# Spacing the steps of scale maxima, moving score maxima of two attention jobs, and giving two elementwise steps to GpSimd in a two-layer hybrid backbone

## The chip, the cores and the metric

The kernel runs on one core of one Trainium2 chip, in one launch. The metric is the device time in microseconds. Before the change the median of three runs is 2726.7 us (2722.78 to 2733.41).

The engines are named as in the profile: PE (TensorE, with its weight loads PEld), DVE (VectorE), ACT (ScalarE), POOL (GpSimd) and SP, whose queue issues nearly all DMAs.

## The reference

Two layers over 2048 latent and 256 context tokens of width 1024. Cut to what is computed:

```python
def hybrid_layer(h, hc, ...):
    lat = split_cols((rms_norm(h, norm_g) * (1.0 + scale) + shift) @ w_in)     # 1024 -> 3584 columns, 15 parts
    cx  = split_cols((rms_norm(hc, norm_g) * (1.0 + scale_c) + shift_c) @ w_in)
    att_l, att_c = gqa_branch(...)      # 4 heads, 2 KV heads, axial rotary, softmax over 2304 keys
    hg_l, hg_c = hgrn_branch(...)       # recurrence, both directions, chunks of 64
    y_conv, y_four, g_att, g_hg = mix_stream(lat, conv_w)   # width-3 convolution; 2-D Fourier; SiLU gates
    y = jnp.concatenate([y_conv, att_l * g_att, hg_l * g_hg, y_four], axis=-1) @ w_out
    h_new = h + gate * y
    # the same for the context stream in layer 0
def attend(qb, k, v):
    s = einsum(q, k) * HEAD_DIM ** -0.5
    p = softmax(s); return einsum(p, v)
# after both layers: rms_norm(h, final_g)
```

## The kernel before

Products that need more than one float16 are made of three float16 products: every operand is split into a high and a low half after it was multiplied by a power of two. That power comes from the largest absolute value of the whole tensor, over all partitions. Its steps are: a maximum along each partition on DVE, a transpose of that column by PE (`rowmax`, L140), a maximum of the row on DVE (L142), a product with ones that spreads the number over all partitions (`spread`, L148), a copy and five small DVE instructions (`pow2`), and then the two split halves (L406 on ACT, L407 on DVE). For the weights `wsplit` does this for each block of 256 columns of `w_in`, 14 blocks a layer.

A layer runs in stages, one after another: the projections and the recurrence (HGRN), its reverse with the Fourier inputs, the Fourier mix, the attention projections, and then four attention jobs. A job is 512 queries. `att_max` forms all scores once with high halves alone and takes their maxima on DVE (L941 on PE into PSUM, L942 on DVE; per job 64 tiles 512 wide and 16 tiles 256 wide). `att_core` forms the scores again transposed, 72 steps per job: two score products (L1016, L1017), the exponential on ACT (L1019), its high half (L1025 on ACT, or L1023 on DVE in the steps that `dve` and `first` name), its low half on DVE (L1026), and four pairs of products with V (L983, L984), which follow four steps later.

Beside the jobs run other streams. Before, in terms of stages: "core 0" is job 0 with the maxima of job 1 and six convolution blocks; "core 1" is job 1 with the maxima of job 2 and the first output tiles; "core 2" is job 2 with the maxima of job 3 and three output tiles; "core 3" is job 3 with four output tiles, and the "tail" is six output tiles (in layer 0 beside the first weights of layer 1). An output tile is 128 tokens: gating (L1266) and splitting of its input (`out_prep`), 48 products 512 wide (L1306), scaling by the gate from PSUM (L1310), the residual add (L1311), and in layer 1 a sum of squares on ACT (L1317). Core 1 begins with `out_open`, which makes the scale of the output's input from six maxima at once (L1599 to L1618).

What sets the order is `weave`: each stream is a generator with a number of units and a share of the stage, and the stream that is furthest behind goes next. A `yield` is a unit's end, so a bare `yield` lets the other streams put their work in between. Instructions then stand in each engine's queue in about that order, and each queue is worked off in order. `paced` makes an instruction wait for the last DVE and ACT instruction recorded before it.

Of the kernel before, what the change touches and what calls it, by code (L numbers as in the profile page):

```python
# [22 lines left out]
D = 1024  # L23
# [49 lines left out]
class Net:  # L73
# [63 lines left out]
    def rowmax(self, a):  # L137
        nc = self.nc
        pt = self.bank("tr")
        nc.tensor.transpose(pt[:1, :128], a, self.id32)  # L140
        m = self.t(self.small, [1, 1], F32, "rowmax")
        nc.vector.tensor_reduce(out=m, in_=pt[:1, :128], axis=AX.X, op=ALU.max)  # L142
        return m

    def spread(self, m):
        nc = self.nc
        pt = self.bank("tr")
        nc.tensor.matmul(pt[:, 0:1], lhsT=self.ones[:1], rhs=m, start=True, stop=True)  # L148
        r = self.t(self.small, [128, 1], F32, "allmax")
        nc.vector.tensor_copy(out=r, in_=pt[:, 0:1])  # L150
        return r
# [23 lines left out]
    def setup(self):  # L175
# [16 lines left out]
        rows = cst.tile([R_N, 128], F32, name="rows")  # L192
# [192 lines left out]
    def wsplit(self, l, b, half, pool=None, pace=False):  # L385
# [532 lines left out]
    def att_fetch(self, job, pool):  # L918
# [4 lines left out]
        Q1 = self.t(pool, [128, 4, 512], F16, "Q1", 2)  # L923
        Q2 = self.t(pool, [66, 4, 512], F16, "Q2", 2)
# [112 lines left out]
    def conv_block(self, l, sb, W, pool):  # L1037
# [33 lines left out]
        th = self.t(pool, [128, 512], F32, "cth", 1)  # L1071
# [187 lines left out]
    def out_prep(self, tt, pool):  # L1259
# [6 lines left out]
        nc.vector.tensor_mul(out=o, in0=o, in1=g)  # L1266
# [10 lines left out]
    def out_tile(self, l, tt, pool):  # L1277
# [23 lines left out]
        for half in range(2):  # L1301
# [9 lines left out]
            nc.vector.tensor_add(out=h[:, c], in0=h[:, c], in1=t)  # L1311
# [38 lines left out]
    def begin(self, pool, nm):  # L1350
# [4 lines left out]
        self.setup()  # L1355
# [20 lines left out]
    def layer(self, l, L, R, tail):  # L1376
# [17 lines left out]
        else:  # L1394
# [11 lines left out]
            weave(tail, (22, start(), 0.2, 0.9))  # L1406
# [5 lines left out]
        with ExitStack() as st:  # L1412
# [3 lines left out]
            if l == 0:  # L1416
                w = [self.wprep(l, b) for b in (8, 9, 10)]
# [29 lines left out]
            for sb in range(1, NS):  # L1447
                weave((33, self.hg_proj(l, sb, hp)), (22, self.hg_levels(l, sb - 1, hp)), (8, norms(sb), 0.3, 1.0), *([(5, self.wprep(l, 13), 0.4, 0.8)] if sb == NS - 1 else []))
# [14 lines left out]
        preps = lambda bs, pool=None: chain(*[(5, self.wprep(l, b, pool, b < 4)) for b in bs])  # L1463
# [6 lines left out]
        with ExitStack() as st:  # L1470
# [33 lines left out]
        jobs[-1]["dve"] = 3  # L1504
# [6 lines left out]
        with ExitStack() as st:  # L1511
# [18 lines left out]
            weave((7, self.att_values(keep, at), 0.02, 0.2), (*chain(*pre, mx(jobs[0])), 0.25, 1.0), part(some[:n]), (*fetch(jobs[1]), 0.6, 0.7))  # L1530
            weave(core(jobs[0]), mx(jobs[1]), part(some[n:]))
# [25 lines left out]
    def out_wmax(self, l):  # L1557
# [14 lines left out]
        self.ows, self.owi = self.pow2(self.allmax(am), self.cst, tag=f"ows{l}")  # L1572
# [14 lines left out]
    def out_open(self, l, pool):  # L1587

        nc = self.nc
        self.gbc = []  # L1590
        for s in range(2 if l < DEPTH - 1 else 1):
            g = self.t(pool, [128, D], F32, f"gbc{s}", 1)
# [8 lines left out]
        pt = self.bank("tr")  # L1601
        nc.tensor.transpose(pt[:6, :128], mx, self.id32)
        m = self.t(self.small, [6, 1], F32, "om6", 1)
        nc.vector.tensor_reduce(out=m, in_=pt[:6, :128], axis=AX.X, op=ALU.max)
        dg = self.t(self.small, [6, 6], F32, "odg", 1)
        nc.vector.tensor_scalar_mul(dg, self.id32[:6, :6], m)
        yield
        pt = self.bank("tr")
        nc.tensor.matmul(pt[:, 0:6], lhsT=self.ones, rhs=dg, start=True, stop=True)
        a = self.t(self.small, [128, 6], F32, "oam", 1)  # L1610
        nc.vector.tensor_copy(out=a, in_=pt[:, 0:6])
# [75 lines left out]
```

## Time and profile before

| | before |
|---|---|
| median of the runs | 2726.7 us |
| the profiled execution, its own time | 2724.91 us |
| its span, first to last instruction | 2721.5 us |
| mean granted TensorE clock | 0.982 |
| busy share of the span: PE, DVE, ACT, POOL | 95%, 79%, 55%, 4% |

The profiled execution is 1.8 us under the median, so differences are taken against 2724.91. A busy share is an average over all stages. A matmul counts as busy from its start to its modelled end, and neighbours overlap, so PE's busy time is read together with the spacing of the starts.

### The profile page before, as it was taken

What the parts mean: (1) busy time and instruction counts of PE and PEld (TensorE: products, weight loads), DVE (VectorE), ACT (ScalarE), POOL (GpSimd) and SP (SyncE); (2) the same over time, 40 slices, a digit from 0 to 9 for tenths busy, and PEclk for the clock granted to TensorE, in tenths of its full rate; (3) what the DMA queues carried; (4) which work ended last, traced back from release to release, by engine and by line L of the source; (5) the groups of instructions that cost most, each with busy time, mean ns of one, the idle gap of its engine ahead of it and who ended that gap; (6) DMA issues with size and microseconds to landing.
All of it is one profiled execution on the core that took longest, in us unless ns stands there. A gap on an engine that the chain in (4) does not pass through costs nothing. (4 is left out here: it accounts for less than half of the span.)

```text
span 2721.5 us, 67137 instructions
## 1 busy us (share of the span) xinstructions
PE 2576.0 (95%) x28046; PEld 1915.2 (70%) x28046; DVE 2147.0 (79%) x4707; ACT 1495.4 (55%) x2789; POOL 105.0 (4%) x108
## 2 busy tenths in 40 slices
PE   6999999999999999999999999999988999999998
PEld 3788877888777875555547888878877787455553
DVE  5888765777698669899877888768678876999885
ACT  2877532322226647798837666423221565879782
POOL 0000001011000000000000000010110000000000
PEclk8999999999999999999999999999999999999999
DMA  6111158353411015224281111344333100423425
GB/s 218 56 49 49 37 187 266 116 152 103 113 38 56 16 45 170 77 72 130 55 247 56 48 49 33 101 131 148 110 92 95 40 25 22 145 79 77 115 52 156
DMA packets 268680, 260.32 MB, mean 96 GB/s; under 512 B 95316, under 2 KB 237656, under 8 KB 268376
## 3 DMA queue, kind: packets, MB, share of 16 engines
q1 hardware_dynamic: 268376, 256.04, 31.5%
q8 instruction: 219, 3.59, 0.5%
q14 instruction: 85, 0.70, 0.1%
HBM read 168.59 MB, written 67.13 MB: 87 GB/s over the span
## 5 line engine op out<-in xcount | busy, mean ns | idle before, releaser
L431 PE MATMUL psmm<-xh,wh 128*128 128x256 f16 x2208 | 608.1, 275 | 7.8 <-DVE xh L357 6.1
L432 PE MATMUL psmm<-xl,wh 128*128 128x256 f16 x2208 | 606.7, 275 | 1.5 <-DVE xl L358 1.5
L433 PE MATMUL psmm<-xh,wl 128*128 128x256 f16 x2208 | 606.5, 275 | 0.7 <-DVE wl L407 0.7
L1019 ACT ACTIVATE aP<-pssc,pshift,ascale 128x512 f32<-128x512 f32 (+1 forms) x584 | 444.6, 778 | 221.6 <-PE pssc L1017 193.2
L445 PE MATMUL psmm<-wh,xh 128*128 128x256 f16 x1664 | 459.1, 276 | 5.6 <-ACT av L818 4.2
L1026 DVE TENSOR_TENSOR apl<-aP,aph 128x512 f16<-128x512 f32 (+1 forms) x584 | 390.2, 681 | 86.8 <-ACT aph L1025 82.6
L446 PE MATMUL psmm<-wl,xh 128*128 128x256 f16 x1664 | 458.4, 275 | 0.0
L447 PE MATMUL psmm<-wh,xl 128*128 128x256 f16 x1664 | 458.2, 275 | 0.0
L942 DVE TENSOR_REDUCE amx<-pstr 128x1 f32<-128x512 f32 (+1 forms) x648 | 391.5, 627 | 46.5 <-PE pstr L941 45.1
L1025 ACT CAST aph<-aP 128x512 f16<-128x512 f32 (+1 forms) x508 | 305.5, 619 | 9.6
L983 PE MATMUL pspv<-V,aph 128*128 128x129 f16 x2320 | 298.7, 221 | 1.4 <-DVE aph L1023 1.2
L984 PE MATMUL pspv<-V,apl 128*128 128x65 f16 x2320 | 269.6, 193 | 4.9 <-DVE apl L1026 3.6
L984 PEld LDWEIGHTS <-apl 128*128 128x128 f16 x2320 | 206.6, 98 | 84.4 <-DVE apl L1026 39.7
L983 PEld LDWEIGHTS <-aph 128*128 128x128 f16 x2320 | 214.6, 97 | 68.5 <-ACT aph L1025 9.4
L431 PEld LDWEIGHTS <-wh 128*128 128x128 f16 x2208 | 217.9, 99 | 59.4 <-issue 7.0
L432 PEld LDWEIGHTS <-wh 128*128 128x128 f16 x2208 | 217.8, 99 | 57.0 <-issue 5.8
L941 PE MATMUL pstr<-K,Q 128*128 128x512 f16 (+1 forms) x648 | 230.0, 362 | 13.3 <-DVE amx L942 8.8
L433 PEld LDWEIGHTS <-wl 128*128 128x128 f16 x2208 | 217.5, 99 | 34.2 <-issue 2.1
L1016 PE MATMUL pssc<-Q,K 128*128 128x512 f16 (+1 forms) x584 | 221.4, 379 | 4.2 <-ACT aP L1019 2.9
L1017 PE MATMUL pssc<-Q,K 66*128 66x512 f16 (+1 forms) x584 | 221.7, 382 | 0.0
L1306 PE MATMUL psmm<-xh,oyh 128*128 128x512 f16 x544 | 206.8, 380 | 1.9 <-DMA oyh<-oa 1.8
L1306 PE MATMUL psmm<-xl,oyh 128*128 128x512 f16 x544 | 206.7, 380 | 0.0
(310 smaller groups left out, 4228.5 us busy)
## 6 DMA issues: line engine op xcount, KB each, us to landing
wst<-w_in SPq DMA_DIRECT2D x56, 512.0 KB
wmod<-w_mod SPq DMA_DIRECT2D x18, 1024.0 KB
d_G<-nh SPq DMA_DIRECT2D x51, 256.0 KB
oo<-d_O SPq DMA_DIRECT2D x34, 384.0 KB
og<-d_G SPq DMA_DIRECT2D x34, 384.0 KB
d_h<-oh SPq DMA_DIRECT2D x18, 512.0 KB
nh<-d_h SPq DMA_DIRECT2D x18, 512.0 KB
nh<-x SPq DMA_DIRECT2D x16, 512.0 KB
```

Of the source, the lines that this page charges most:

```text
L431: nc.tensor.matmul(out, lhsT=wh[:, k, cs], rhs=a, start=(k == 0), stop=False)
L432: nc.tensor.matmul(out, lhsT=wh[:, k, cs], rhs=b, start=False, stop=False)
L433: nc.tensor.matmul(out, lhsT=wl[:, k, cs], rhs=a, start=False, stop=(k == KC - 1))
L445: nc.tensor.matmul(out, lhsT=a, rhs=wh[:, k, :], start=(k == 0), stop=False)
L446: nc.tensor.matmul(out, lhsT=a, rhs=wl[:, k, :], start=False, stop=False)
L447: nc.tensor.matmul(out, lhsT=b, rhs=wh[:, k, :], start=False, stop=(k == KC - 1))
L942: nc.vector.tensor_reduce(out=mx[:, h, j, i : i + 1], in_=ps[:, :w], axis=AX.X, op=ALU.max)
L983: nc.tensor.matmul(pv(j), lhsT=ph[:, t], rhs=self.V[:, s, kv, :], start=st, stop=False, skip_group_check=True)
L984: nc.tensor.matmul(pv(j)[:, 0:65], lhsT=pl[:, t], rhs=self.V[:, s, kv, 0:65], start=False, stop=sp and j % 2 == 1, skip_group_check=True)
L1019: nc.scalar.activation(out=P[:, :n], in_=ps[:, :n], func=AF.Exp, scale=self.ascale, bias=self.pshift)
L1026: nc.vector.tensor_sub(out=pl[:, :n], in0=P[:, :n], in1=ph[:, :n])
L1306: nc.tensor.matmul(ps, lhsT=y, rhs=w, start=(i == 0), stop=(i == len(mms) - 1))
```

## The change

Five things change.

1. `wsplit` has two more bare yields between its steps (not where `quick` is set, that is at the start of layer 0), and `rowmax` is no longer paced; the stream's unit counts grow from 5 to 7. `out_wmax` and `out_open` get such units too. The maximum of the values (`att_vmax`) is taken among the last gate blocks of the attention projections, before it was taken at the start of the stage after.
2. The score maxima of job 2 stand in core 0, behind those of job 1, and those of job 3 in core 1. Q's tiles have three buffers. Job 2, as job 3, now makes 27 of its 72 high halves on DVE (`dve` = 3).
3. The gating product of `out_prep` and the residual add of `out_tile` are GpSimd's.
4. The output tiles are split at 5, 9, 13 (before 5, 8, 12): core 2 gets four, the tail five.
5. Several small tiles lie in other buffers (`rows`, the gate rows, `cth`).

```diff
     def rowmax(self, a):
+        n = a.shape[1]
         pt = self.bank("tr")
-        nc.tensor.transpose(pt[:1, :128], a, self.id32)
+        nc.tensor.transpose(pt[:n, :128], a, self.id32)
...
-    def wsplit(self, l, b, half, pool=None, pace=False):
+    def wsplit(self, l, b, half, pool=None, pace=False, quick=False):
...
         yield
-        with slow():
-            m = self.rowmax(am)
-        yield
+        if not quick:
+            yield
+        m = self.rowmax(am)
+        yield
+        if not quick:
+            yield
...
+    def att_vmax(self):
+        am = self.t(self.small, [128, 1], F32, "vam", 1)
+        self.nc.vector.tensor_reduce(out=am, in_=self.vmax, axis=AX.X, op=ALU.max)
+        yield
+        m = self.rowmax(am)
+        yield
+        self.vscale, self.visc = self.pow2(self.spread(m), self.cst, tag="avs")
+        yield
...
-        Q1 = self.t(pool, [128, 4, 512], F16, "Q1", 2)
-        Q2 = self.t(pool, [66, 4, 512], F16, "Q2", 2)
+        Q1 = self.t(pool, [128, 4, 512], F16, "Q1", 3)
+        Q2 = self.t(pool, [66, 4, 512], F16, "Q2", 3)
...
-        th = self.t(pool, [128, 512], F32, "cth", 1)
+        th = self.t(pool, [128, 512], F32, "cc", 3)
...
-        nc.vector.tensor_mul(out=o, in0=o, in1=g)
+        nc.gpsimd.tensor_tensor(out=o, in0=o, in1=g, op=ALU.mult)
...
-            nc.vector.tensor_add(out=h[:, c], in0=h[:, c], in1=t)
+            nc.gpsimd.tensor_tensor(out=h[:, c], in0=h[:, c], in1=t, op=ALU.add)
...
-            weave(tail, (22, start(), 0.2, 0.9))
+            weave(tail, (30, start(), 0.2, 0.9))
...
-        jobs[-1]["dve"] = 3
+        jobs[-1]["dve"] = jobs[-2]["dve"] = 3
...
-            weave(core(jobs[0]), mx(jobs[1]), part(some[n:]))
+            run(fetch(jobs[2])[1])
+            weave(core(jobs[0]), chain(mx(jobs[1]), mx(jobs[2])), part(some[n:]))
...
-        T = (5, 8, 12)
-        run(fetch(jobs[2])[1])
+        T = (5, 9, 13)
+        run(fetch(jobs[3])[1])
         weave(
             core(jobs[1]),
-            (*mx(jobs[2]), 0.05, 1.0),
-            (*chain((1, self.out_load(l, t0, ou)), *[(1, self.out_weights(k)) for k in (6, 7)], (3, self.out_open(l, ou))), *((0.0, 0.04) if need else (0.055, 0.08))),
-            (*out(range(t0, T[0])), 0.07 if need else 0.09, 1.0),
+            (*mx(jobs[3]), 0.05, 1.0),
+            (*chain(*[(1, self.out_weights(k)) for k in (6, 7)], (4, self.out_open(l, ou)), (1, self.out_load(l, t0, ou))), *((0.0, 0.08) if need else (0.02, 0.11))),
+            (*out(range(t0, T[0])), 0.12 if need else 0.14, 1.0),
         )
-        run(fetch(jobs[3])[1])
-        weave(core(jobs[2]), (*mx(jobs[3]), 0.05, 1.0), out(range(T[0], T[1])))
+        weave(core(jobs[2]), out(range(T[0], T[1])))
```

On PE at the border of core 0 and core 1 of layer 0, before: L1602 is the transpose of the six maxima and L1609 the product that spreads them, L983 and L984 are products with V, L941 score maxima.

```order
L984 MATMUL pspv_14068<-V_10661,apl_14585 128x65
L1602 MATMUL pstr_14684<-id_90,omx_2055_14681 6x128
L1609 MATMUL pstr_14690<-odg_14688,ones 128x6
L941 LDWEIGHTS Q_2040_14628
L941 MATMUL pstr_14756<-K_1393_10659,Q_2040_14628 128x512
```

The two stood next to each other, and ten score-maxima products followed before the next step of the core. After the change the same product (now L155; its transpose, L142, stands 71 rows ahead of it) has core steps (L998 and L999 with V, L1031 and L1032 scores) around it, and the score maxima (L956) alternate with them:

```order
L998 MATMUL pspv_15008<-V_10679,aph_14948 128x129
L999 LDWEIGHTS apl_14949
L999 MATMUL pspv_15008<-V_10679,apl_14949 128x65
L1031 LDWEIGHTS K_1402_10677
L1031 MATMUL pssc_15065<-Q_1519_11403,K_1402_10677 128x512
L155 MATMUL pstr_14983<-odg_14956,ones 128x6
L956 LDWEIGHTS Q_2128_14886
L956 MATMUL pstr_15005<-K_1402_10677,Q_2128_14886 128x512
L1032 LDWEIGHTS K_1403_10678
```

So PE has other work between the transpose and the product that needs DVE's answer. On DVE in the middle of core 2 of layer 0 the maxima (L942) alternated with the low halves (L1026) before:

```order
L1026 TENSOR_TENSOR apl_17253<-aP_17250,aph_17252 128x512
L942 TENSOR_REDUCE amx_16671<-pstr_17256 128x1
L1026 TENSOR_TENSOR apl_17276<-aP_17273,aph_17275 128x512
L942 TENSOR_REDUCE amx_16671<-pstr_17279 128x1
L1026 TENSOR_TENSOR apl_17296<-aP_17293,aph_17295 128x512
```

After it the low halves (L1041) stand there with the high halves that DVE now makes (L1038) and the output tiles' scaling (L1325):

```order
L1041 TENSOR_TENSOR apl_17458<-aP_17455,aph_17457 128x512
L1038 CAST aph_17478<-aP_17476 128x512
L1041 TENSOR_TENSOR apl_17479<-aP_17476,aph_17478 128x512
L1041 TENSOR_TENSOR apl_17499<-aP_17496,aph_17498 128x512
L1041 TENSOR_TENSOR apl_17519<-aP_17516,aph_17518 128x512
```

No maxima are left in core 2. In core 0 of layer 0, DVE had one such reduction for each low half, with a convolution's steps among them; now it has two (L957), as here:

```order
L957 TENSOR_REDUCE amx_13349<-pstr_14036 128x1
L1041 TENSOR_TENSOR apl_14024<-aP_14021,aph_14023 128x512
L957 TENSOR_REDUCE amx_13349<-pstr_14045 128x1
L957 TENSOR_REDUCE amx_13349<-pstr_14071 128x1
L1041 TENSOR_TENSOR apl_14062<-aP_14059,aph_14061 128x512
L957 TENSOR_REDUCE amx_13349<-pstr_14086 128x1
L1082 SCALAR_TENSOR_TENSOR cu_14115<-psmm_13997,ds_9613,cc_13995 128x2x256
```

## Rows read from the trace of the kernel before

**Rows 1.** The page, its first part: busy time, share of the span and number of instructions of each engine.

```profile
PE 2576.0 (95%) x28046; PEld 1915.2 (70%) x28046; DVE 2147.0 (79%) x4707; ACT 1495.4 (55%) x2789; POOL 105.0 (4%) x108
```

**Rows 2.** Busy time in stretches: core 0, 1, 2, 3 and tail of layer 0, then the same of layer 1. Columns: the stretch in us from the span's start, its length, busy us and number of instructions of each engine, the granted clock, DMA's share and GB/s.

```profile
810.00:1008.70 198.70, 198.57 (x1941) 158.44 (x1940) 144.98 (x277) 117.69 (x175) 0.00 (x0) 1.00 0.08 28
1008.70:1147.80 139.10, 131.60 (x1049) 71.58 (x1046) 125.77 (x235) 101.90 (x154) 0.15 (x1) 0.96 0.41 124
1147.80:1259.40 111.60, 109.11 (x949) 61.43 (x946) 103.76 (x188) 96.70 (x154) 0.00 (x0) 1.00 0.29 80
1259.40:1364.00 104.60, 103.43 (x944) 58.44 (x942) 85.02 (x160) 83.12 (x128) 0.00 (x0) 1.00 0.37 102
1364.00:1437.00 73.00, 68.83 (x324) 32.32 (x322) 54.95 (x114) 23.07 (x38) 1.62 (x5) 0.98 0.75 228
2107.50:2310.10 202.60, 202.14 (x1947) 159.59 (x1946) 153.17 (x288) 117.98 (x174) 0.00 (x0) 1.00 0.08 26
2310.10:2427.80 117.70, 111.87 (x951) 61.61 (x948) 114.45 (x222) 98.90 (x159) 1.54 (x2) 0.97 0.36 106
2427.80:2542.60 114.80, 109.31 (x950) 60.86 (x948) 110.77 (x205) 100.06 (x167) 1.96 (x3) 1.00 0.28 78
2542.60:2650.80 108.20, 105.23 (x943) 57.83 (x941) 88.39 (x168) 87.06 (x144) 3.09 (x4) 1.00 0.37 99
2650.80:2721.50 70.70, 62.18 (x289) 27.99 (x286) 38.35 (x64) 15.43 (x35) 3.85 (x7) 0.96 0.53 154
```

**Rows 3.** The waits of PE for the steps of scale maxima: waiting line, what it waited for, us in total, times, the longest. The first two are of the stretch 100 to 760 us (layer 0, past its start), the other two of 1440 to 2107 us (layer 1).

```profile
PE pstr L148 <- DVE rowmax L142: 9.4, 3, 3.8
...
PE pstr L140 <- DVE wam L391: 2.0, 1, 2.0
...
PE pstr L140 <- DVE wam L391: 10.2, 3, 4.5
PE pstr L148 <- DVE rowmax L142: 9.6, 4, 2.7
```

**Rows 4.** The same columns as Rows 2 for eight stretches in which the granted clock fell to its lower level, each right behind a wait of PE: the first of the eight, the two at the start of a core 1, and the sum (length first).

```profile
675.20:678.60 3.40, 3.40 (x19) 2.34 (x17) 2.19 (x6) 0.84 (x2) 0.00 (x0) 0.50 0.41 100
...
1013.10:1023.40 10.30, 8.46 (x21) 2.55 (x20) 9.30 (x26) 2.61 (x4) 0.00 (x0) 0.50 0.77 264
...
2317.00:2323.80 6.80, 5.64 (x14) 1.75 (x13) 5.91 (x18) 1.93 (x3) 0.00 (x0) 0.50 0.90 309
sum 41.00, PE 35.72 PEld 19.79 DVE 33.67 ACT 12.91 POOL 0.00; mean PE 4.47 PEld 2.47 DVE 4.21 ACT 1.61 POOL 0.00
```

**Rows 5.** The timeline of PE in core 0 of layer 0 (start, us, engine, line, operation): a product 512 wide and its successor, one 256 wide and its successor, and the first product with V of three successive pairs (first and last).

```profile
880.01 0.38 PE L1017 MATMUL pssc<-Q,K 66*128 66x512 f16 x1
880.23 0.27 PE L431 MATMUL psmm<-xh,wh 128*128 128x256 f16 x1
...
880.56 0.27 PE L431 MATMUL psmm<-xh,wh 128*128 128x256 f16 x1
880.67 0.27 PE L432 MATMUL psmm<-xl,wh 128*128 128x256 f16 x1
...
882.31 0.22 PE L983 MATMUL pspv<-V,aph 128*128 128x129 f16 x1
...
882.49 0.22 PE L983 MATMUL pspv<-V,aph 128*128 128x129 f16 x1
```

**Rows 6.** Groups by line and shape, over the whole span: line, engine, operation, out<-in, shapes, count, busy us, mean ns of one, idle us before them and what ended it.

```profile
L1026 DVE TENSOR_TENSOR apl<-aP,aph 128x512 f16<-128x512 f32 x576 | 387.2, 685 | 86.8 <-ACT aph L1025 82.6
L942 DVE TENSOR_REDUCE amx<-pstr 128x1 f32<-128x512 f32 x512 | 340.2, 683 | 34.2 <-PE pstr L941 32.9
...
L942 DVE TENSOR_REDUCE amx<-pstr 128x1 f32<-128x256 f32 x136 | 56.2, 416 | 12.3 <-PE pstr L941 12.2
...
L1311 DVE TENSOR_TENSOR oh<-oh,ot 128x512 f32<-128x512 f32 x68 | 46.5, 684 | 0.4
...
L1266 DVE TENSOR_TENSOR oo<-oo,og 128x768 f32<-128x768 f32 x34 | 32.2, 952 | 8.8 <-DMA oo<-d_O 8.7
...
L1023 DVE CAST aph<-aP 128x512 f16<-128x512 f32 x76 | 31.0, 421 | 3.0 <-ACT aP L1019 2.9
```

**Rows 7.** The same columns, the groups of POOL alone. L171 is a power (exponent -0.5).

```profile
L171 POOL TENSOR_TENSOR arr<-arv,mhalf 128x12 f32<-128x12 f32 (+1 forms) x18 | 42.3, 2349 | 369.3 <-DVE arv L169 293.8 <-DVE p2e L123 75.5
L171 POOL TENSOR_TENSOR nrr<-nrv,mhalf 128x1 f32<-128x1 f32 x52 | 31.6, 607 | 1166.9 <-DVE nrv L169 1134.1 <-DVE arc L998 32.8
...
L188 POOL MEMSET cact<- 128x256 f32 x1 | 0.3, 317 | 0.0
...
masks.py:199 POOL TENSOR_SCALAR_AFFINE_SELECT id<-id 128x128 f32<-128x128 f32 x1 | 0.3, 296 | 0.0
```

**Rows 8.** The timeline at the end of the span: the last residual add and the sum of squares behind it.

```profile
2713.74 0.69 DVE L1311 TENSOR_TENSOR oh<-oh,ot 128x512 f32<-128x512 f32 x1
2714.80 0.63 ACT L1317 ACTIVATE ot<-oh 128x512 f32<-128x512 f32 x1 [4.74 <-DVE oh L1311]
```

More of the change, by code (lines that the diff above doesn't have):

```diff
@@ L138, in rowmax @@
         nc = self.nc
+        n = a.shape[1]
         pt = self.bank("tr")
[L140 to L143 removed]
+        nc.tensor.transpose(pt[:n, :128], a, self.id32)
+        m = self.t(self.small, [6, 1], F32, "rowmax")
+        nc.vector.tensor_reduce(out=m[:n], in_=pt[:n, :128], axis=AX.X, op=ALU.max)
+        if n == 1:
+            return m[:1]
+        dg = self.t(self.small, [6, 6], F32, "odg", 1)
+        nc.vector.tensor_scalar_mul(dg[:n, :n], self.id32[:n, :n], m[:n])
+        return dg[:n, :n]
     def spread(self, m):
         nc = self.nc
+        n = m.shape[1]
         pt = self.bank("tr")
[L148 to L150 removed]
+        nc.tensor.matmul(pt[:, 0:n], lhsT=self.ones[:n], rhs=m, start=True, stop=True)
+        r = self.t(self.small, [128, n], F32, f"allmax{n}")
+        nc.vector.tensor_copy(out=r, in_=pt[:, 0:n])
         return r
@@ L191, in setup @@
         self.masks = cst.tile([128, 6, 64], U16, name="masks")
-        rows = cst.tile([R_N, 128], F32, name="rows")
+        rows = self.t(pool, [R_N, 128], F32, "rows", 1)
         def put(r0, src):
@@ L366, in new_x, with wprep @@
         return self.t(pool, [128, KC, n], F16, f"xh{i}", 1), self.t(pool, [128, KC, n], F16, f"xl{i}", 1)
-    def wprep(self, l, b, pool=None, pace=False):
+    def wprep(self, l, b, pool=None, pace=False, quick=False):
         half = self.wload(l, b)
         yield
-        yield from self.wsplit(l, b, half, pool, pace)
+        yield from self.wsplit(l, b, half, pool, pace, quick)
     def wload(self, l, b):
@@ L1362, in begin @@
             if i == 2:
-                run(self.wsplit(0, 7, half))
+                run(self.wsplit(0, 7, half, quick=True))
             run(self.mod_cols(0, x, w[i], mod, pool, "mm"))
@@ L1416, in layer @@
             if l == 0:
-                w = [self.wprep(l, b) for b in (8, 9, 10)]
+                w = [self.wprep(l, b, quick=True) for b in (8, 9, 10)]
                 with self.after(last):
@@ L1490, in layer, with one @@
             self.att_open(l, ab)
+            vm = self.att_vmax()
+            def one(g):
+                next(g)
+                yield
             weave(
@@ L1493, in layer @@
                     merge(gates(6, 0, some[6:]) + gates(11, 256, some[:-3]), [(17, self.att_block(l, sb)) for sb in range(NS)]),
-                    late(), *gates(11, 256, some[-3:]),
+                    late(), *[x for sb in some[-3:] for x in (*gates(11, 256, [sb]), (1, one(vm)))],
                 ),
-                chain((10, self.out_wmax(l)), preps((1, 2, 3, 0), wc)),
+                chain((12, self.out_wmax(l)), preps((1, 2, 3, 0), wc)),
             )
@@ L1529, in layer @@
             part = lambda sbs: chain(*[x for sb in sbs for x in conv[sb]])
-            weave((7, self.att_values(keep, at), 0.02, 0.2), (*chain(*pre, mx(jobs[0])), 0.25, 1.0), part(some[:n]), (*fetch(jobs[1]), 0.6, 0.7))
-            weave(core(jobs[0]), mx(jobs[1]), part(some[n:]))
+            weave((5, self.att_values(keep, at), 0.02, 0.2), (*chain(*pre, mx(jobs[0])), 0.25, 1.0), part(some[:n]), (*fetch(jobs[1]), 0.6, 0.7))
+            run(fetch(jobs[2])[1])
+            weave(core(jobs[0]), chain(mx(jobs[1]), mx(jobs[2])), part(some[n:]))
         wcs.close()
@@ L1571, in out_wmax @@
         nc.vector.tensor_reduce(out=am, in_=mx, axis=AX.X, op=ALU.max)
-        self.ows, self.owi = self.pow2(self.allmax(am), self.cst, tag=f"ows{l}")
+        yield
+        m = self.rowmax(am)
+        yield
+        self.ows, self.owi = self.pow2(self.spread(m), self.cst, tag=f"ows{l}")
         yield
@@ L1600, in out_open @@
         nc.vector.tensor_reduce(out=mx[:, 5:6], in_=self.vmax, axis=AX.X, op=ALU.max)
[L1601 to L1606, printed above, removed]
         yield
[L1608 to L1611, printed above, removed]
+        m = self.rowmax(mx)
+        yield
+        a = self.spread(m)
         b = self.t(self.small, [128, 4], F32, "obd", 1)
```

19 lines of the change are left out of this document (8 added, 11 removed).

## The prediction

> **What bounds the kernel now.** I read the busy shares first. PE is busy 95% of the span, DVE 79%, POOL 4% [rows 1]; so a gain must come from PE's time, and DVE's work is worth something only where it holds PE up. PE's busy time counts overlapping matmuls, so next I took what PE needs at least from the spacing of starts: 0.22 us for a product 512 wide (880.01 to 880.23), 0.11 us for one 256 wide, 0.09 us for a pair of products with V (0.18 us over two pairs) [rows 5]. A step of a core is two 512-wide products and four pairs, 0.80 us, and 72 of them 57.6 us. A job's score maxima are 64 x 0.22 + 16 x 0.11 = 15.8 us. An output tile is 48 x 0.22 = 10.6 us.
>
> Third, the stages [rows 2]. In core 0 PE is busy in 198.6 of 198.7 us and 202.1 of 202.6: PE alone bounds it, and DVE has 28% and 24% to spare. Core 1 needs 57.6 + 15.8 + 5 x 10.6 = 126.4 us of PE in layer 0 and takes 139.1; with three tiles 105.2 and 117.7 in layer 1. Core 2 needs 105.2 and takes 111.6 and 114.8, with DVE busy 93% and 96%. Core 3 needs 57.6 + 4 x 10.6 = 100.0 and takes 104.6 and 108.2. So some 12.6 us are lost in each core 1, 6 to 10 in each core 2, 5 to 8 in each core 3, almost none in core 0.
>
> Last, the waits and the clock. Outside the start of layer 0, PE waits 9.4 + 2.0 + 10.2 + 9.6 = 31.2 us in eleven places for the steps of scale maxima [rows 3]. Behind several of them, and at both starts of core 1, the granted clock is at 0.50 (1.2 GHz) for 41.0 us in all; the two core 1 pieces are 10.3 and 6.8 us of it, so 23.9 us stand elsewhere [rows 4]. At 0.50 PE does half the work, so those 23.9 us cost up to 12.
>
> **The change part by part.** The sum goes against the profiled execution's 2724.9 us, 1.8 under the median.
>
> *Spaced steps.* No instruction is added; between a maximum and the PE instruction that needs it there now stand one or two more units of the other stream. A wait is 0.7 to 4.5 us long, 2.8 on average (31.2 over 11), and a unit of the main stream is at most six products, several of which pass for one of the weights' units; in the order I count 2 to 3 us more PE work between the transpose and the product with ones. I take 28 of the 31.2 us as gone; at worst, if DVE answers later by as much, only a third is gone. What is late next is the split itself, but its weights are used a block later. Of the half-clock 23.9 us I take two thirds of the 12, -8; below that 0, above it -12. The values' maximum lies in the same stretch and is in these numbers.
>
> *Core 0.* It gains 15.8 us of PE in each layer, in full, since PE has no gap there. It also gains 64 x 0.683 + 16 x 0.416 = 50.4 us of reductions [rows 6]: DVE has then 195.4 of 214.5 us (91%) in layer 0 and 203.6 of 218.4 (93%) in layer 1. Core 2 shows what such a share costs: 96% of DVE with 10 us over PE's need, where ACT too was at 87%. ACT is at 59% here, so I take 4 us of collisions: +20 a layer; 16 at least, and 30 where each of six convolution blocks, whose four to six DVE instructions stand in a row, holds PE up for 2.5 us.
>
> *Core 1.* PE's work stays (job 3's maxima for job 2's). Its loss is at the start: in 10.3 us PE ran 21 matmuls at the lower clock while DVE was busy 9.3 us [rows 4], because ten score-maxima products stood ahead of the core's steps and each waited for a reduction of 0.68 us. These now alternate with core steps. DVE also loses 0.952 + 2 x 0.684 = 2.32 us a tile to GpSimd [rows 6], 11.6 us in layer 0 and 7.0 in layer 1. Of the 12.6 us lost I take 9 and 8 back; 3 at least.
>
> *Core 2.* It becomes what core 3 was: 72 steps, 27 high halves on DVE (27 x 0.421 = 11.4 us), four tiles, no maxima. Core 3 takes 104.6 and 108.2 us [rows 2], so core 2 gains 7.0 and 6.6 by that row alone; with 9.3 us less on DVE I take 8 and 10. Core 3 keeps its work and loses the same 9.3 us of DVE, which had 81% there: -1 and -3.
>
> *Tails.* Each loses a tile of 10.6 us. In layer 1 nothing else is there: -10.6, and the last residual add, now GpSimd's, ends later by its extra length (0.69 us on DVE [rows 8], about 1.2 below): -10. In layer 0 the weights of layer 1 run beside it, DVE is at 75% and DMA at 75% [rows 2]; with 2.4 + 5 x 2.3 us less on DVE that goes to PE's length too: -9; if the loads decide, 0.
>
> *GpSimd's length.* No row shows it multiply or add. Its shortest full-width row is a memset, 317 ns for 256 columns, 1.2 ns each; an affine select costs 296 for 128, 2.3 each; the only two-input rows are powers, from 607 ns for one column to 2349 for mostly twelve, 158 ns each [rows 7]. The power's price belongs to the power, since the same engine does 128 columns of the select in half of one column's power; the select is nearest. So 1.8 us for 768 columns and 1.2 for 512, and a tile has P = 4.2 us on POOL, with 2.2 by the memset. A tile comes every 10.6 us at the fastest, so POOL, idle else, keeps up, and the product waits there for its DMA where DVE had waited 8.7 us [rows 6]. Behind the add in layer 1 stands ACT's sum of squares, and behind that the exponentials: 0.5 us more twice a tile, in queues with 13 to 20% idle. I take +2 for all of it. GPSIMD Engine Reference (the Trainium skill), section "Elementwise — side-by-side cycle accounting", gives 4497 ns for an add of 2048 columns, by which P would be an estimated 3.9 us and the sum the same; no run here shows it.
>
> *At nothing:* tiles in other buffers, `rowmax` for six rows (the same instructions as `out_open` had), an earlier fetch of Q (three DMAs on SP, idle at a stage's border).
>
> Sum: layer 0, +20 - 9 - 8 - 1 - 9 = -7; layer 1, +20 - 8 - 10 - 3 - 10 = -11; waits -28, clock -8, GpSimd +2: -52. 2724.9 - 52 = 2673.
>
> **The rivals.** (A) *GpSimd holds DVE up, and the kernel is slower.* If a DVE instruction that reads two SBUF operands can't run beside a GpSimd one that does, each tile gives DVE P instead of taking 2.32 off it. Core 1 then has 114.2 + 5P and 107.5 + 3P of DVE, cores 2 and 3 about 76 + 4P and 79 + 4P. With P = 4.2 core 1 becomes 135 and 120, +5 and +10 on my 130 and 110: 2688. It decides from about P = 8 us (4.5 ns a column): core 1 154 and 132, cores 2 and 3 108 and 111, +65 in all: 2738, slower. For it: L1026, 0.685 us in each of the 72 steps [rows 6], is such an instruction. Against: that P is twice the select's. SBUF — State Buffer (the Trainium skill), "Who interferes with whom", states just this lock: the second of the two blocks until the first ends. Its price by rows is this rival's; the trace of before has only powers of a few columns on POOL there and can't show it.
>
> (B) *DVE becomes core 0's bound.* If it costs there what core 1 of layer 0 shows at the worst, 139.1 us for 125.8 us of DVE [rows 2], a factor 1.106, core 0 is 216 and 225, little over mine; with the 2.5 us at every block as well it is +15 a layer: 2703. For it, the order (two reductions a step, convolution steps between); against, that PE's work in between grows too.
>
> (C) *The waits only move.* If DVE answers later by as much as the added units are long, two thirds of the 28 + 8 stay: 2673 + 24 = 2697. For it: the spaced reductions stand behind the same DVE queue. Against: the waits are short, 4.5 us at most [rows 3].
>
> **How the numbers follow.** The sum has 0.62, A 0.12, B 0.12, C 0.14. A change under 0.5% (13.6 us, 2713 to 2740) is about what a measurement of this kernel can't tell from none. My own case is faster in nearly all its spread (2650 to 2700), B and C at 2697 to 2703 with spreads over 2713 in a third of them, A half within and half slower, and some of A beyond: faster 0.79, same 0.10, slower 0.11. The likeliest case's own range is 2650 to 2697. For 8 in 10 I go down to 2645 (all waits and clock, core 1 at PE's need) and up to 2718, which holds B, C and the mild end of A.
>
> **What would show it.** In the new profile: the waits of PE for `rowmax` and `wam` under 8 us in sum, and few stretches at 0.50; core 0 at 216 to 224 us; core 1 at 130 and 110; core 2 within 2 us of core 3; the last tail at 60. DVE's low halves still 685 ns each beside GpSimd's products of about 1.8 us; if they are longer, or idle DVE stands before them with POOL as the releaser, A is at work. The forecast is wrong if core 0 grows by over 30 us, or if the eleven waits come back under other names.

## The result, and the profile after

The changed kernel takes 2755.2 us (median of 4 runs, 2753.4 to 2762.4), the kernel before on the same chip 2730.1. The ratio is 1.010, with a 95% interval of 1.0068 to 1.0131: slower by one per cent, where 2673 was forecast. The profiled execution took 2757.0 us, its span 2755.2.

The page's first line, which answers to [rows 1]:

```profile
PE 2574.2 (93%) x28046; PEld 1919.1 (70%) x28046; DVE 2175.6 (79%) x4669; ACT 1478.6 (54%) x2725; POOL 269.8 (10%) x210
```

PE has the same matmuls and the same busy time, in a longer span. DVE was to lose work to POOL: it has 38 instructions fewer (the 102 that went to POOL, less 64 high halves of job 2 that came from ACT) and is busy 28.6 us longer. The stages, as in [rows 2] (core 0, 1, 2, 3 and tail of layer 0, then of layer 1; stretch, length, busy us of PE, weight loads, DVE, ACT and POOL, the clock, DMA's share and GB/s):

```profile
813.70:1031.80 218.10, 216.53 (x2024) 166.58 (x2023) 189.37 (x363) 119.27 (x175) 0.00 (x0) 1.00 0.09 30
1031.80:1172.00 140.20, 130.21 (x1049) 71.45 (x1047) 125.52 (x220) 102.25 (x154) 24.94 (x17) 0.99 0.40 115
1172.00:1280.60 108.60, 101.51 (x916) 58.16 (x913) 83.65 (x136) 85.53 (x126) 19.12 (x13) 0.98 0.34 93
1280.60:1392.20 111.60, 101.52 (x942) 59.13 (x940) 83.39 (x140) 85.00 (x125) 19.21 (x12) 1.00 0.31 91
1392.20:1455.00 62.80, 56.93 (x259) 25.99 (x257) 49.30 (x94) 22.16 (x36) 23.40 (x19) 0.95 0.79 243
2114.90:2335.60 220.70, 218.81 (x2028) 167.73 (x2027) 196.70 (x372) 118.68 (x174) 0.00 (x0) 1.00 0.08 26
2335.60:2458.40 122.80, 111.41 (x954) 62.13 (x951) 116.00 (x218) 101.60 (x160) 18.20 (x12) 0.99 0.33 97
2458.40:2573.50 115.10, 103.89 (x917) 59.01 (x915) 88.65 (x148) 88.99 (x142) 22.15 (x17) 0.97 0.31 88
2573.50:2688.90 115.40, 103.81 (x941) 59.30 (x938) 90.40 (x152) 87.71 (x141) 22.23 (x16) 0.99 0.30 88
2688.90:2755.20 66.30, 53.47 (x240) 23.62 (x238) 24.59 (x41) 13.47 (x30) 25.70 (x21) 0.95 0.47 143
```

Core 0 grew by 19.4 and 18.1 us, as forecast. Core 2 has now only 84 to 89 us of DVE, and PE still idles 7 and 11 us in it. Against the forecast, the loss is in the stages in which POOL works and DVE makes low halves, cores 1 to 3, and to a lesser part in the tails. DVE's groups, as in [rows 6] (L1041 is the low half, L957 the score maxima, L1038 DVE's high half, L1285 the low part of a gated tile, L1325 the scaling of an output tile):

```profile
L1041 DVE TENSOR_TENSOR apl<-aP,aph 128x512 f16<-128x512 f32 x576 | 423.3, 741 | 97.1 <-ACT aph L1040 88.4 <-PE pssc L1032 1.3
L957 DVE TENSOR_REDUCE amx<-pstr 128x1 f32<-128x512 f32 x512 | 338.8, 683 | 35.0 <-PE pstr L956 33.7
...
L1038 DVE CAST aph<-aP 128x512 f16<-128x512 f32 x140 | 67.3, 489 | 2.5 <-ACT aP L1034 2.1
...
L1325 DVE TENSOR_TENSOR ot<-psmm,xh 128x512 f32<-128x512 f32 x68 | 46.7, 686 | 25.0 <-PE psmm L1321 24.7
...
L1285 DVE SCALAR_TENSOR_TENSOR ob<-oo,osc,oa 128x768 f16<-128x768 f32 x34 | 41.5, 1224 | 32.5 <-ACT oa L1284 32.5
```

The low half went from 685 to 741 ns and DVE's high half from 421 to 489. The reduction and the scaling, whose large input lies in PSUM, stayed at 683 and 686. POOL's two new groups (compare [rows 7]):

```profile
L1326 POOL TENSOR_TENSOR oh<-oh,ot 128x512 f32<-128x512 f32 x68 | 98.9, 1454 | 524.6 <-DVE ot L1325 485.4 <-DVE ams L964 12.2 <-ACT aph L1040 10.8
L1281 POOL TENSOR_TENSOR oo<-oo,og 128x768 f32<-128x768 f32 x34 | 65.8, 1946 | 405.1 <-DVE apl L1041 321.9 <-DMA oo<-d_O 28.5 <-DMA og<-d_G 20.7
```

So P is 1.95 + 2 x 1.45 = 4.85 us a tile, 0.65 over the 4.2 used. What one tile does in core 3 of layer 0, in the timeline (start, us, engine, line, out<-in; in brackets the idle time ahead and its releaser):

```profile
1296.85 1.58 DVE L1285 SCALAR_TENSOR_TENSOR ob<-oo,osc,oa 128x768 f16<-128x768 f32 x1 [2.67 <-ACT oa L1284]
1297.53 0.38 PE L1031 MATMUL pssc<-Q,K 128*128 128x512 f16 x1 [1.28 <-ACT aP L1034]
...
1297.57 1.98 POOL L1326 TENSOR_TENSOR oh<-oh,ot 128x512 f32<-128x512 f32 x1
...
1298.35 1.75 DVE L1041 TENSOR_TENSOR apl<-aP,aph 128x512 f16<-128x512 f32 x1
...
1300.02 0.41 DVE L1038 CAST aph<-aP 128x512 f16<-128x512 f32 x1
...
1300.15 0.20 PE L999 MATMUL pspv<-V,apl 128*128 128x65 f16 x1 [1.32 <-DVE apl L1041]
...
1300.21 0.78 ACT L1034 ACTIVATE aP<-pssc,pshift,ascale 128x512 f32<-128x512 f32 x1 [0.97 <-DVE apl L1041]
...
1301.28 0.68 DVE L1041 TENSOR_TENSOR apl<-aP,aph 128x512 f16<-128x512 f32 x1
```

POOL's add runs to 1299.55. The low half that starts in it takes 1.75 us and ends 0.55 after it; the next one, with POOL free, takes 0.68. PE (products with V) and ACT (the next exponential, whose buffer the low half still reads) each wait for it by name. PE's two groups that wait, over the span (scores, and products with the low half):

```profile
L999 PE MATMUL pspv<-V,apl 128*128 128x65 f16 x2320 | 269.7, 194 | 16.1 <-DVE apl L1041 15.2
...
L1031 PE MATMUL pssc<-Q,K 128*128 128x512 f16 x576 | 219.9, 382 | 32.6 <-ACT aP L1034 31.6
```

Before, the same waits were 3.6 and 2.9 us. The waits for the steps of scale maxima, which were 31.2 us in [rows 3], did go (stretches 100 to 760 and 1440 to 2114 us):

```profile
PE pstr L142 <- DVE wam L398: 2.6, 1, 2.6
PE pstr L142 <- DVE wam L398: 5.0, 2, 3.7
```

### The profile page after: what moved, and what is told of

It is laid out like the page before. It is cut to its first block, busy times and chain, and to the rows that moved or that the text cites. A ratio compares the mean times of both kernels' runs of the same rounds, so it can differ in the third digit from the quotient of the medians.

```text
span 2755.2 us, 67284 instructions
## 1 busy us (share of the span) xinstructions
PE 2574.2 (93%) x28046; PEld 1919.1 (70%) x28046; DVE 2175.6 (79%) x4669; ACT 1478.6 (54%) x2725; POOL 269.8 (10%) x210
## 5 line engine op out<-in xcount | busy, mean ns | idle before, releaser
L1041 DVE TENSOR_TENSOR apl<-aP,aph 128x512 f16<-128x512 f32 (+1 forms) x584 | 426.3, 737 | 97.1 <-ACT aph L1040 88.4
L957 DVE TENSOR_REDUCE amx<-pstr 128x1 f32<-128x512 f32 (+1 forms) x648 | 390.5, 627 | 46.6 <-PE pstr L956 44.6
L998 PE MATMUL pspv<-V,aph 128*128 128x129 f16 x2320 | 291.9, 222 | 0.7 <-DVE aph L1038 0.6
L999 PE MATMUL pspv<-V,apl 128*128 128x65 f16 x2320 | 269.7, 194 | 16.1 <-DVE apl L1041 15.2
L1040 ACT CAST aph<-aP 128x512 f16<-128x512 f32 (+1 forms) x444 | 269.0, 613 | 10.8
L999 PEld LDWEIGHTS <-apl 128*128 128x128 f16 x2320 | 208.2, 98 | 92.2 <-DVE apl L1041 37.9
L441 PEld LDWEIGHTS <-wh 128*128 128x128 f16 x2208 | 218.1, 99 | 66.3 <-issue 12.6
L998 PEld LDWEIGHTS <-aph 128*128 128x128 f16 x2320 | 216.2, 98 | 61.4 <-issue 4.8
L1031 PE MATMUL pssc<-Q,K 128*128 128x512 f16 (+1 forms) x584 | 222.1, 380 | 32.6 <-ACT aP L1034 31.6
L956 PE MATMUL pstr<-K,Q 128*128 128x512 f16 (+1 forms) x648 | 228.9, 359 | 25.0 <-DVE amx L957 17.9
L1032 PE MATMUL pssc<-Q,K 66*128 66x512 f16 (+1 forms) x584 | 222.7, 382 | 0.0
```

Source lines behind the costliest of these rows:

```text
L441: nc.tensor.matmul(out, lhsT=wh[:, k, cs], rhs=a, start=(k == 0), stop=False)
L957: nc.vector.tensor_reduce(out=mx[:, h, j, i : i + 1], in_=ps[:, :w], axis=AX.X, op=ALU.max)
L998: nc.tensor.matmul(pv(j), lhsT=ph[:, t], rhs=self.V[:, s, kv, :], start=st, stop=False, skip_group_check=True)
L999: nc.tensor.matmul(pv(j)[:, 0:65], lhsT=pl[:, t], rhs=self.V[:, s, kv, 0:65], start=False, stop=sp and j % 2 == 1, skip_group_check=True)
L1041: nc.vector.tensor_sub(out=pl[:, :n], in0=P[:, :n], in1=ph[:, :n])
```

## The experiments

The theory was A, the lock (L in the expectations): a DVE instruction that reads two operands in SBUF can't run beside a GpSimd one that reads SBUF. Its rivals were waits (W: GpSimd's longer product and add stand in each tile's own chain, and queues wait for their results) and the order (tile split, moved maxima). Ratios are to the kernel before on the same chip.

**e1: both steps back on DVE.** The rest of the change is kept.

```diff
-        nc.gpsimd.tensor_tensor(out=o, in0=o, in1=g, op=ALU.mult)
+        nc.vector.tensor_mul(out=o, in0=o, in1=g)
...
-            nc.gpsimd.tensor_tensor(out=h[:, c], in0=h[:, c], in1=t, op=ALU.add)
+            nc.vector.tensor_add(out=h[:, c], in0=h[:, c], in1=t)
```

> The changed kernel with the gating product and the residual add back on DVE; all else as changed. Theory G (the two steps on GpSimd cost what was lost): core 2 and 3 fall from 108.6 to 115.4 us to about 102, both cores 1 to about 132 and 112, the tail of layer 1 to 61; in all about 2695, clearly below both kernels. Rival M (the moved score maxima and core 0 lose it): cores 1 to 3 stay where they are after the change and the time stays at 2745 to 2760.

Measured: 2698.4 us, 0.9887 (0.9864 to 0.9910). So all of the change but the two steps ("the order" below) gains 32 us, and GpSimd's two steps cost 57. By stages (us, from the windows of the profiled runs; "forecast" is the prediction's term applied to before):

```
                   before  forecast  after    e1
l0 core 0           198.7   218.7    218.1  218.0
l0 core 1           139.1   130.1    140.2  133.9
l0 core 2           111.6   103.6    108.6  102.5
l0 core 3           104.6   103.6    111.6  102.4
l1 core 0           202.6   222.6    220.7  220.6
l1 core 1           117.7   109.7    122.8  113.0
l1 core 2           114.8   104.8    115.1  102.5
l1 core 3           108.2   105.2    115.4  106.6
l1 tail              70.7    60.7     66.3   63.5
```

Cores 1 to 3 of both layers sum to 713.7 us after and 660.9 in e1: 52.8 of the 61.8 us between the spans. In the same six rows PE is busy 652.4 and 640.9 us, so 41.3 of the 52.8 are idle PE, and 11.5 are PE's longer busy time, in part at a lower mean clock (0.97 against 1.00 in core 2 of layer 1, where e1's row is this):

```profile
2420.80:2523.30 102.50, 99.99 (x917) 57.84 (x914) 85.72 (x167) 89.07 (x142) 3.05 (x4) 1.00 0.34 99
```

**e2: e1, and GpSimd does the same products and adds beside it, into a scratch tile that nobody reads.**

```diff
+        scr = self.t(pool, [128, 768], F32, "scr", 1)
+        nc.gpsimd.tensor_tensor(out=scr, in0=o, in1=g, op=ALU.mult)
         nc.vector.tensor_mul(out=o, in0=o, in1=g)
```

(and an add of 512 columns behind each residual add.)

> The kernel of e1_dve with GpSimd instructions added that write a scratch tile nobody reads: behind each gating product one product of 768 columns of the same operands, behind each residual add one add of 512 columns. DVE, ACT and PE wait for none of them. It does 102 GpSimd instructions more than the computation needs. Theory L (a DVE instruction with two operands in SBUF can't run beside a GpSimd one that reads SBUF): low halves beside them take about 1.3 us in place of 0.69, and most of the gap between e1_dve and the changed kernel is there, some 30 to 45 us over e1_dve. Rival W (the loss is ACT's and DVE's waits for GpSimd's results): within 10 us of e1_dve.

Measured: 2776.7 us, 1.0166 (1.0144 to 1.0188), 78 us over e1, though no result is waited for, and more than the 30 to 45 that were expected. This run tells the lock from waits for results. Its groups of DVE:

```profile
L1041 DVE TENSOR_TENSOR apl<-aP,aph 128x512 f16<-128x512 f32 x576 | 417.0, 731 | 72.9 <-ACT aph L1040 65.5 <-PE pssc L1032 1.9
L957 DVE TENSOR_REDUCE amx<-pstr 128x1 f32<-128x512 f32 x512 | 339.2, 684 | 33.1 <-PE pstr L956 31.9
L1038 DVE CAST aph<-aP 128x512 f16<-128x512 f32 x140 | 82.0, 596 | 4.5 <-ACT aP L1034 4.3
```

And its two groups of PE that wait:

```profile
L999 PE MATMUL pspv<-V,apl 128*128 128x65 f16 x2320 | 271.6, 195 | 37.4 <-DVE apl L1041 31.9 <-DVE nrv L176 4.7 <-DVE p2e L124 0.3
...
L1031 PE MATMUL pssc<-Q,K 128*128 128x512 f16 x576 | 221.0, 384 | 16.4 <-ACT aP L1034 15.5
```

In e1 the same three groups are these:

```profile
L1041 DVE TENSOR_TENSOR apl<-aP,aph 128x512 f16<-128x512 f32 x576 | 391.7, 686 | 79.3 <-ACT aph L1040 73.1 <-PE pssc L1032 0.9
...
L999 PE MATMUL pspv<-V,apl 128*128 128x65 f16 x2320 | 267.7, 193 | 10.2 <-DVE apl L1041 9.5 <-DVE p2e L124 0.3
...
L1031 PE MATMUL pssc<-Q,K 128*128 128x512 f16 x576 | 218.7, 380 | 8.0 <-ACT aP L1034 6.5
```

In e2 PE waits first for the low half itself. In the changed kernel two thirds of the wait come by way of ACT: its exponentials stand in one queue with the high half of a gated tile (L1284), which waits 56 us for POOL's product, where in e1 it waits 35 for DVE's. Not all of e2's 78 us need be the stop: the scratch steps also hold a tile's buffers and POOL's queue. DVE's waits for a tile's loads went from 11.2 us in e1 to 18.2, and those of layer 1's last step for a power from POOL from 8.2 to 13.2, 12 us in all.

**e3 and e4: one step of the two on GpSimd.** e3 has e1's first edit alone (adds stay on GpSimd), e4 its second (products stay there).

> The changed kernel with only the gating product back on DVE, the residual adds stay on GpSimd. Theory W: ACT's waits for the gating product (56.1 us in the changed kernel) go, and the time falls by 25 us or more, to 2730 or less. Theory L by GpSimd's busy time: 66 of its 165 us go, so 40% of the gap to e1_dve, about 2735.

> The changed kernel with only the residual adds back on DVE, the gating product stays on GpSimd. Theory W: the waits for the gating product stay, the sums of squares no longer wait: 10 to 15 us less than the changed kernel, about 2743. Theory L by busy time: 99 of 165 us go, 60% of the gap to e1_dve, about 2720.

Measured: 2733.6 (1.0016, 1.0000 to 1.0031) and 2743.5 (1.0045, 1.0027 to 1.0063). Over e1 the adds alone cost 35 us and the products alone 45, together 57: they are not additive, and each alone already eats the whole gain of the order.

e3 came out where L put it (2735), but e4 where W did (2743) and not at L's 2720. PE's waits say the same (us, from the same two groups of PE in each run):

```
                          e1   after    e2    e3    e4
for the low half (L999)   9.5   15.2   31.9  19.6   8.5
by way of ACT (L1031)     6.5   31.6   15.5  15.4  29.2
```

e4's two groups:

```profile
L999 PE MATMUL pspv<-V,apl 128*128 128x65 f16 x2320 | 270.9, 194 | 9.3 <-DVE apl L1041 8.5 <-DVE p2e L124 0.3
L1031 PE MATMUL pssc<-Q,K 128*128 128x512 f16 x576 | 221.1, 384 | 30.4 <-ACT aP L1034 29.2
```

And ACT's wait for the product in e4, then in e1:

```profile
ACT oa L1284 <- POOL oo L1281: 74.1, 26, 11.4
...
ACT oa L1284 <- DVE oo L1281: 35.4, 16, 10.3
```

With the products alone PE waits for low halves no longer than in e1, and ACT's exponentials don't either (17.4 and 17.7 us), but PE waits by way of ACT nearly as in the changed kernel. A product takes 2.01 us in e4 on average and 1.80 at its shortest, against 0.95 on DVE, so most of what it is longer is its own length and not a stop. So waiting for the product costs time beside the lock: e2 shows the one, e4 the other. How the 57 us divide, no run separates.

**e5: GpSimd only writes.** e1 with memsets of a scratch tile on GpSimd (three for each product, three for each add).

> The kernel of e1_dve with GpSimd instructions at the places of e2_dve_beside that only write: three memsets of 768 columns behind each gating product, three of 512 behind each residual add, on a scratch tile nobody reads; they are work that the computation needs none of. Theory L (the lock is on reads): within 6 us of e1_dve, 2698, and the low halves stay at 0.69 us. Rival B (any GpSimd work beside DVE slows it, by SBUF bandwidth or writes): 20 us or more over e1_dve.

Measured: 2707.2 us, 0.9909 (0.9882 to 0.9937), 9 over e1, past L's 6 and far from the rival's 20, with more GpSimd time (185 us) than the products and adds had (165). One of its two groups of memsets on POOL:

```profile
L1334 POOL MEMSET scr<- 128x512 f32 x204 | 108.6, 532 | 11.7
```

And the low halves:

```profile
L1041 DVE TENSOR_TENSOR apl<-aP,aph 128x512 f16<-128x512 f32 x576 | 392.8, 688 | 79.8 <-ACT aph L1040 74.2
```

The memsets ran bunched in the two core 1 stages and not at their tiles, so this is a test beside core 1's DVE alone. Of the 576 low halves 112 overlap a memset by the timeline's times: 687 ns on average, 688 for the others. A GpSimd that only writes doesn't hold them up. Of DVE's high halves only six overlap a memset, and two of them took 651 and 868 ns where the others take 422; for these the run doesn't say the same. The 9 us over e1 are not explained; 5.7 us of the longer span lie in core 1 of layer 1, beside the memsets, where PE waits 4.3 us for score maxima against 0.2 in e1.

**e6 and e7: the spaced steps by themselves.** e6 is the kernel before with all of the change that concerns the steps of scale maxima (yields, weights of the streams, the unpaced `rowmax`, one for all, the earlier maximum of the values); the small tiles' buffers and Q's third one, which add no work, are in it too. e7 is e1 with the bare yields of `wsplit` off:

```diff
     def wsplit(self, l, b, half, pool=None, pace=False, quick=False):
+        quick = True
```

(the weights of four streams go back with it.)

> The kernel before with the spaced steps alone (the bare yields, the unpaced row maximum, the earlier maximum of the values, four units of out_open); score maxima, tile split and GpSimd as before. My prediction had 36 us for it: 2690. The stages of e1_dve say that 23 us are won in the reverse and attention projections and 13 lost in the Fourier stage and at the first score maxima: about 2718.

> The kernel of e1_dve without the bare yields of the weights' scale (unit counts 5 again). If the spacing is worth what the stages of e1_dve say, 9 us more than e1_dve, about 2707; by my prediction's 36 us, 2734; if the waits only moved, 2698 as e1_dve.

Measured: e6 2709.5 (0.9923, 0.9898 to 0.9947), a gain of 20 where the prediction's two terms say 36; e7 2703.0 (0.9896, 0.9875 to 0.9917), 4.6 over e1 and within its interval. The named waits fell to 6.3 us in both e1 and e6, and to 14.0 in e7, so most of their fall comes from the other parts and not from the bare yields. By the profiled spans e6 gains 13.5. These are the stretches from the first product of the recurrence to core 0, layer 0 and 1, in the kernel before and then in e6:

```profile
85.00:810.00 725.00, 692.97 (x9248) 588.78 (x9248) 549.46 (x1338) 322.03 (x738) 45.26 (x35) 0.98 0.36 109
...
1487.60:2107.60 620.00, 576.33 (x7758) 497.95 (x7758) 491.30 (x1233) 259.22 (x575) 39.14 (x29) 0.98 0.30 89
...
84.50:812.50 728.00, 694.91 (x9248) 588.55 (x9248) 550.54 (x1338) 321.89 (x738) 45.37 (x35) 0.98 0.37 109
...
1491.10:2096.10 605.00, 573.96 (x7759) 496.95 (x7759) 490.42 (x1233) 258.78 (x575) 39.13 (x29) 0.98 0.32 92
```

Layer 1 gained 15.0 us, layer 0 lost 3.0. There PE's waits for scale steps fell by 8.8 us, and others grew by as much: a wait at the first score maxima that the profile names "issue" (4.0, none before; in e1, where it is 3.9, it names the load of Q), score maxima on DVE (+1.9), `av` on ACT (+1.6), `cu` on DVE (+1.5). The granted clock is 0.98 in all four.

**e8: the product issued at the load**, ahead of need, to take its length out of the tile's chain.

> The changed kernel with GpSimd's gating product issued where its operands are loaded, in place of just ahead of the ACT instruction that reads it. Theory W: ACT's 56 us of waits for it fall under 20 and the time by 25 us or more, to 2730. Theory L: the products still stand beside DVE's low halves, the time stays within 12 us of the changed kernel, 2743 to 2765.

Measured: 2757.8 (1.0098, 1.0072 to 1.0124). ACT's waits for the product did not fall (58.6 us in 24 places, 56.1 in 22 before the edit), so the run doesn't test what it was made for. It shows only that an earlier place in the program is no cure.

**e9: e1 with `wsplit`'s yields off for blocks 5 and 11** beside the Fourier steps. From the first Fourier transpose to ACT's copy of the first attention values (`av`) the kernel before takes 69.3 and 66.5 us in layer 0 and 1, e1 71.8 and 73.7.

> e1 (both GpSimd steps back on DVE) with the bare yields of the scale steps left out for the two blocks prepared beside the Fourier stage (5 and 11) alone, and kept elsewhere. From the first Fourier matmul to the first attention block, e1 takes 71.8 and 73.6 us, the kernel before 69.3 and 66.5. If the yields cost there because the split lands next to the Fourier steps, this kernel gives back some 6 us: about 2692. If that stretch is long for another reason (the order of what came before it), it is e1 within 2 us: 2698. The lock says nothing here.

Measured: 2695.2 (0.9883, 0.9864 to 0.9903). That stretch is now 68.9 and 68.4 us, so the yields did cost there, but the total moved by 3 us, which the intervals can't tell from none; at layer 1's first score maxima PE now waits 5.3 us for a convolution step on DVE (`cy`) where it waited 1.3 in e1. e9 has the fastest median of all, and e1 is its equal.

**e10: GpSimd in the tails alone.**

```diff
-        nc.gpsimd.tensor_tensor(out=o, in0=o, in1=g, op=ALU.mult)
+        (nc.gpsimd if tt >= 14 else nc.vector).tensor_tensor(out=o, in0=o, in1=g, op=ALU.mult)
```

(and the adds with tt >= 13. That is four products and five tiles' adds in each tail, not the two tiles that the expectation names.)

> The changed kernel with GpSimd used for the two tiles of each tail alone (gating of tiles 14 and 15, adds of 13 to 15 by their index), where no low halves are left; everything ahead on DVE. Lock theory: there is little DVE work with two SBUF operands to hold up in a tail, so the time is e1's within 5 us, 2695 to 2704, and cores 1 to 3 as in e1 (133.9, 102.5, 102.4; 112.9, 102.5, 106.6). Length theory (what costs is the longer product and add in each tile's own chain, wherever it stands): each tail grows by what it grew from e1 to the changed kernel, 3 us, and with a quarter of the tiles a quarter of the 57 us comes back: about 2712.

Measured: 2703.5 (0.9909, 0.9889 to 0.9929), 5 us over e1, at the upper edge of what the lock theory allowed and far from the other's 2712. Cores 1 to 3 are e1's to 2 us. The tail of layer 1 is this:

```profile
2635.00:2701.10 66.10, 53.63 (x240) 23.76 (x238) 25.20 (x42) 13.47 (x30) 23.95 (x20) 0.93 0.48 143
```

That is the changed kernel's 66.3, against 63.5 in e1: without low halves beside it GpSimd's length costs some 3 us in the last tail (1 to 2 in layer 0's), the whole of what the tails lost. The rest of the 57 is made where the cores run. Whether by the lock or by ACT's waits this run doesn't say, since a tail has neither low halves nor exponentials.

**e11: the kernel before with the two GpSimd steps alone.**

> The kernel before with the gating products and residual adds on GpSimd and nothing else changed. Lock theory: 4.85 us of GpSimd a tile stop DVE, which is busy 90 to 97% in its cores 1 and 2, so the loss is about that of e1 against the changed kernel (57) or more: 2775 to 2800. Theory that the loss is made only by the new order (tile split, maxima moved, DVE's high halves in core 2): within 15 us of the kernel before, 2715 to 2745.

Measured: 2779.6 (1.0188, 1.0169 to 1.0208), 53 us slower. So it isn't the new order that makes the steps dear (53 with the old one, 57 with the new): order alone -32, GpSimd alone +53, both +25.

## Why the prediction was wrong

**What held.** Core 0: +20 a layer forecast, +19.4 and +18.1 measured, so B (DVE becomes its bound) didn't come. Cores 1 to 3 without GpSimd (e1): within 4 us of the forecast in each, and their sum with core 0 +2.8 and -0.6 a layer, where the terms say +2 and -1. In part this is luck: core 3's -1 and -3, and some of core 1's and 2's, were argued from 2.32 us a tile that DVE would lose, and in e1 DVE loses nothing; core 3 got 2.2 and 1.6 us shorter all the same. The named waits: under 8 us forecast, 7.6 measured. The tail of layer 0: from its start to the next recurrence 123.6 us before, 114.0 in e1, as the -9 said.

**What failed first: the step "GpSimd's length ... +2 for all of it", and with it A's price, "It decides from about P = 8 us".** The lock of A is real, with 0.12 on it, and the sign named for it came: the low halves rose to 741 ns. P came out at 4.85, near the estimate, and yet GpSimd cost 57 us. The +2 has two holes. It takes DVE as free beside GpSimd, which a stopped low half (1297 ns on average) refutes. And of the waits for results it counts only the adds' before the sum of squares: the product ahead of ACT's high half, in one queue with the exponentials, is given no wait but that for its DMA, and e4 shows PE waiting 29.2 us by way of ACT with products alone, against 6.5 in e1. The false step in A is that a stage costs the larger of PE's need and DVE's sum. With P = 4.85 that rule gives core 1 114.2 + 5 x 4.85 = 138.5 and 107.5 + 3 x 4.85 = 122.1 us (140.2 and 122.8 measured, which is luck: DVE is busy 125.5 and 116.0 us of them, stops included), but for cores 2 and 3 95 to 98, under PE's need, so nothing lost; they lost 6 to 13 us each against e1. DVE's idle share there (17 us of 102.5 in e1's core 2 of layer 1) doesn't soak up a stop: a low half stopped for 0.6 us on average, and up to 1.6, stands in a step of 1.4 us (102.5 over 72), PE's queue has the products with it next (PE stood for 1.32 us in the timeline above), and ACT needs the buffer that it still reads. In the six stages POOL's busy time less e1's powers is 118.5 us for 52.8 us lost, 0.45 us per us; in e2 119.8 for 71.5, 0.60; by the whole times the adds alone come to 0.34 (35 over 102 us) and the products alone to 0.67 (45 over 68). So there is no one price, and none of these is what an engine's sum of work gives.

The evidence could have been weighed better: every low half [rows 6] reads two SBUF tensors and stands in the chain of each step, so the condition of A held in every step in which a tile was gated. The trace left open whether the lock exists.

**What failed second: the waits of the scale steps (-28) and the clock (-8).** The waits went, the time only in part: 13.5 us by spans, 20 by medians. In layer 0 this is C, in another form than it was put: other waits of the same stretch took the place. In layer 1 idle PE fell from 43.7 to 31.0 us and busy PE by 2.4; in layer 0 neither fell. The clock gave next to nothing: it is 0.98 in these stretches before and in e6, and in e1 too. The last tail gave 7.2 us in e1 for the 10 forecast.

Together, by the profiled spans: without GpSimd's +2 the sum says -54, and e1 has -28. Of the 26 that are missing, 24 are in the second (36 forecast, 12 measured in e1's two stretches) and 3 in the last tail. The first adds 57. Two readings were off by a little. A job with `dve` = 3 makes 32 of its 72 high halves on DVE, not 27 (the 76 of [rows 6] are twice 32 and 6), so core 2 took on 13.5 us and not 11.4; and DVE has 27% to spare in core 0 of layer 0, not 28. No term rests on either.

## What to carry to other kernels

Before moving an elementwise step from VectorE to GpSimd, list the VectorE instructions that will run beside it: if those on the critical chain read two SBUF tensors, or are fast SBUF casts, the move can cost more than it takes off, as here, even where VectorE is idle a fifth of the time. Look for what a stop or a longer step holds up in the chain, and not at busy shares; and see which queue waits for the moved step's result, and what stands behind it there. And when a named wait is removed, ask what PE would wait for next in the same stretch before taking the whole wait as gain.

## What the hardware showed

The trace of before couldn't show the lock; these runs show it and where it ends. Sorted by whether they overlap a GpSimd product or add by more than 0.1 us (worked out from the times of all rows of the changed kernel's trace): low halves 686 ns clear (524) and 1297 beside (52, up to 2303); DVE's high halves 419 (112) and 769 (28); the low part of a gated tile 1009 (21) and 1572 (13). Not touched: the 512-wide reductions from PSUM, 683 (491) and 680 (21). How long a stop lasts is as regular: of the 37 low halves that start inside such a GpSimd step 35 end 0.55 us after it ends, whether they took 0.8 us or 2.3; the eight high halves 0.28 to 0.29 us after it, the twelve gated low parts 0.81 to 0.82. So DVE goes on when the GpSimd step is done. GpSimd pays too: a product takes 1.80 us at its shortest and up to 2.53, an add 1.26 and up to 2.24. SBUF — State Buffer (the Trainium skill), "Who interferes with whom", draws just these borders: two SBUF inputs against a GpSimd instruction that reads, casts in a fast mode too (DVE's high halves, 421 ns where a low half as wide takes 685), and not an instruction with at most one SBUF input outside the fast modes; here they agree, and e5 agrees, for the low halves, that a GpSimd instruction which only writes doesn't contend with two SBUF inputs.

GPSIMD Engine Reference (the Trainium skill), "Elementwise — side-by-side cycle accounting", gives 4497 ns for an add of 2048 columns; scaled by columns, product and add would be an estimated 1.69 and 1.12 us. The shortest rows are 1.80 and 1.26, some tenth of a microsecond more.
